# Mixture of experts in token blocks of 32, 32 and 64 instead of 64 and 64, with the first block in four column tiles

## The chip, the cores and the metric

The kernel runs on one core of one Trainium2 chip. The metric is the device time of one execution in microseconds, median of the runs. TensorE (PE) multiplies, VectorE (DVE), ScalarE (ACT) and GpSimd (POOL) work on vectors, SyncE (SP) issues most transfers; each engine runs its own instructions in order, and engines wait for each other by semaphores.

## The reference

One block of a flow model: three parallel token mixers over 256 latent tokens (and 256 context tokens), a merge, a layer norm; then a mixture of experts over the 256 tokens, and another layer norm. Only the mixture is touched here:

```python
def moe_ffn(h, w_router, b_router, w_gate_up, b_gate_up, w_down, b_down):   # h: 256 x 1024
    top_val, top_idx = lax.top_k(h @ w_router + b_router, 4)                # 32 experts
    probs = jax.nn.softmax(top_val, axis=-1)
    ...
    def expert(acc, xs):                                                    # for each of the 32
        gate, up = jnp.split(h @ wgu + bgu, 2, axis=-1)                     # wgu: 1024 x 2048
        gate = jnp.minimum(gate, 7.0)
        up = jnp.clip(up, -7.0, 7.0)
        y = ((up + 1) * gate * jax.nn.sigmoid(1.702 * gate)) @ wd + bd      # wd: 1024 x 1024
        return acc + cw[:, None] * y, None
```

All in f32; the weights of an expert are 12.58 MB. Only a token that chose an expert counts for it. The reference's own inputs send these numbers of tokens to experts 0 to 31 (1,024 in all, 32 on average):

```
17 34 33 47 48  4 19 77   8 46 101 48 28 12 11 40
25  1 46 42 36  8 28 31  44 14  21 64 12 39 32  8
```

So 17 experts have at most 32 tokens, 13 have 33 to 64, experts 7 and 10 have more, and none has over 128.

## The kernel before

The mixers take the first 300 us or so. The rest is a loop over the 32 experts, written out, in the order of the code on every engine (lines 1479 to 1552). The token matrix `h2` stays on the chip. For each expert, 64 slots are filled: `select` (L1359, VectorE) compares each token's place in its expert's list with the slot numbers, `gather` (L1363) multiplies the tokens with this 0/1 matrix on TensorE and scales the product on ScalarE (L1370). Slots for two experts are selected together, two experts ahead.

The expert itself: `gate_up` (L1388) with the slots as the stationary operand, 64 columns, and the weights streaming 512 wide. Two such products, on PSUM partitions 0 to 63 and 64 to 127, form one bank of gate and up; there are two banks (halves 0 and 1 of the hidden size), so two rounds of 16 products. In the trace each f32 product is two records, so a round is 32 records. `act` (L1395) is the clamped SwiGLU of a bank, four VectorE operations and one of ScalarE. `turn` (L1403) transposes the result on TensorE and copies it on ScalarE, `down` (L1410) is 16 products. `spread` (L1416) scales the bank by the tokens' routing weights and splits it in two rounded parts (VectorE, ScalarE, VectorE), and `scatter` (L1421) adds them to the 256 tokens in four PSUM banks, eight products. `spots` (L1373) makes the scatter's matrix and the weights: VectorE scales, TensorE transposes, VectorE compares and sums. It stands between two parts of the second round (L1510). `biases` (L1385) starts each bank with one product. The banks: `gbank` two for gate/up and down, alternating, `sbank` two for everything small.

An expert with over 64 tokens runs a second body, `over`, for 64 more, in two branches (`tc.If`, L1503 `rest_gate` and L1518 `rest`), which TensorE, VectorE and ScalarE skip otherwise. Behind the last expert stands a loop for experts with over 128 tokens (L1557), skipped here.

Weights: SyncE issues them in the order of `queue` (L139 to 145) by `pump` (L148), six transfers of 2 MB per expert (four gate/up, two down), each into a pair of slots of 1 MB. There are 18 slots: 14 in the large arena, two each in `A2` and `A3`. The transfer into a pair waits for the last reader of what was there: `done` frees gate/up pairs 0 and 1 behind the first branch (L1505), pairs 2 and 3 behind the second (L1520), the down pairs in the middle and at the end of `down`. The end of the kernel (L1571 to 1600) takes statistics of the four banks, normalizes and writes four pieces out.

Of the kernel before, what the change touches and what calls it, by code (L numbers as in the profile page):

```python
# [117 lines left out]
def kernel(ctx, tc, x, cx, cols, rows, csts, wsm, wgt, bada, brt, sgub, bdn, bgu,  # L118
# [21 lines left out]
    for e in range(NE):  # L140
        queue += [(("gu", e, i), wgu[e, i]) for i in range(4)]
        if e < NE - 1:
            queue += [(("dn", e, i), wdn[e, i]) for i in range(2)]
        else:
            queue += [(("dn1", e, i), wdn[e, i // 2][:, 2048 * (i % 2):2048 * (i % 2) + 2048]) for i in range(4)]
    loaded = {}

    def pump():  # L148
        while queue:
# [11 lines left out]
            nc.sync.dma_start(out=s, in_=src)  # L161
# [63 lines left out]
    with ExitStack() as p1:  # L225
# [1050 lines left out]
        bgr = Buf(A2, 2, 512)  # L1276
        nc.sync.dma_start(out=bgr[:], in_=bgu.rearrange("p (h n) -> p h n", h=2))
# [6 lines left out]
        bsel = Buf(A2, NE, 2)  # L1284
# [19 lines left out]
        S.copy(out=bst[:], in_=bgr[:])  # L1304
        G.memset(bsel[:], 0.0)
        for r in range(4):
            S.copy(out=bsel[32 * r:32 * r + 32, :, r % 2], in_=ident[32 * r:32 * r + 32, 32 * r:32 * r + 32])
        G.tensor_tensor(out=bst[64:128], in0=bgr[64:128], in1=bst[64:128].bitcast(F32), op=ALU.subtract)
# [36 lines left out]
    def chunk():  # L1345
        return dict(sT=Buf(R, 256), cwv=Buf(A2, 2), gT=Buf(A2, KB, SLOTS), gc=[Buf(A2, 256)])

    yhx, ylx = Buf(R, 512), Buf(R, 512)
    cur, over = chunk(), chunk()
    over["gc"] = over["gc"] + cur["gc"]  # L1350
    cur["gc"] = cur["gc"] + [Buf(A2, 256)]
    ysum = Buf(A2, 512)
    up, sg = ysum[:, 0:256], ysum[:, 256:512]
    sw = ysum[:, 0:256].rearrange("p (t a n) -> p t a n", t=2, a=2)
# [18 lines left out]
    def spots(b, sl, e):  # L1373
        for t in range(2):
            V.tensor_scalar_mul(sw[:, t], sl[:, t, :].unsqueeze(1).to_broadcast([P, 2, SLOTS]), cw[:, t, e:e + 1])
        pw = sps2()
        for t in range(2):
            T.transpose(pw[:, P * t:P * t + P], sw[:, t].rearrange("p a n -> p (a n)"), ident[:])  # L1378
# [3 lines left out]
    def bias_of(e):  # L1382
        V.tensor_copy(out=bse[e % 2][:].rearrange("p (q n) -> p q n", q=2), in_=bsel[:, e, :].unsqueeze(2).to_broadcast([P, 2, SLOTS]))  # L1383

    def biases(e, hf, pg):  # L1385
        mm(pg[:], bse[e % 2][:], bst[:, hf, :], start=True, stop=False, skip_group_check=True)  # L1386

    def gate_up(hT, pg, ks, w):  # L1388
        for k in ks:
            wk = w[k // 2].rearrange("p (k n) -> p k n", k=2)  # L1390
            for q in range(2):
                mm(pg[64 * q:64 * q + 64, :], hT[:, k, :], wk[:, k % 2, 512 * q:512 * q + 512], start=False, stop=k == KB - 1,  # L1392
                   skip_group_check=True)

    def act(b, hf, pg):  # L1395
        gc = b["gc"][hf]
        V.tensor_scalar_min(gc[:], pg[:, 0:256], LIMIT)  # L1397
        S.activation(out=sg[:], in_=gc[:], func=AF.Sigmoid, scale=SW_ALPHA)  # L1398
        V.tensor_scalar(out=up[:], in0=pg[:, 256:512], scalar1=LIMIT, scalar2=-LIMIT, op0=ALU.min, op1=ALU.max)
        V.tensor_tensor(out=gc[:], in0=gc[:], in1=sg[:], op=ALU.mult)  # L1400
        V.scalar_tensor_tensor(out=gc[:], in0=up[:], scalar=1.0, in1=gc[:], op0=ALU.add, op1=ALU.mult)

    def turn(b, hf):  # L1403
# [3 lines left out]
        S.copy(out=b["gT"][:, 4 * hf:4 * hf + 4, :].rearrange("p (q j) n -> p j q n", q=2),  # L1407
               in_=pt[:, 0:256].rearrange("p (j q n) -> p j q n", j=2, q=2))

    def down(b, py, ks, w):  # L1410
        for k in ks:
            wk = w[k // 2].rearrange("p (k n) -> p k n", k=2)
# [66 lines left out]
    for e in range(NE):  # L1479
# [11 lines left out]
        if e:  # L1491
            scatter(cur)
# [188 lines left out]
```

## Time and profile before

| | |
|---|---|
| median of 3 runs | 1285.31 us (1282.2 to 2010.12) |
| the profiled execution | 1286.55 us, its span 1284.7 us |
| TensorE busy | 1189.9 us, 93% |
| TensorE weight loads busy | 611.3 us, 48% |
| VectorE busy | 461.2 us, 36% |
| ScalarE busy | 284.5 us, 22% |
| moved | 471.74 MB, mean 367 GB/s |

Times in the rows are microseconds from the start of the span. A row of the timeline is a run of like instructions: start, time from the first start to the last end, engine, line, operation, tiles (out <- in), shape, count, and in brackets how long the engine had been idle and what ended that. `PE` is a product, `PEq` a branch or the like on TensorE's sequencer, `SPq` an issue of a transfer. `128*64` is the tile of the array that a product uses: rows by columns. `PEclk`, the granted clock, is a mean over a window; 1.00 is 2.4 GHz.

### The profile page before, as it was taken

The page shows a single profiled execution, that of the slowest core. Times are in us where ns is not written, and L with a number is a line of the kernel's source. Part 1 is how long each engine was busy: PE and PEld are TensorE (multiplying, and loading weights), DVE is VectorE, ACT ScalarE, POOL GpSimd, SP SyncE. Part 2 cuts the span into 40 slices and gives each one's busy share as a digit, 9 for nine tenths or more (in the row PEclk, how much of TensorE's full clock was granted, in tenths as well). Part 3 has the DMA queues.
Part 4 walks back from the last instruction along what each step waited for, and adds up shares of the span by engine and source line. Part 5 has one row for each costly group of instructions (what it writes and reads, how often), then busy time and mean ns, then how long its engine had stood idle before and what let it go on. Part 6 is the DMA issues. An engine that isn't in the chain of part 4 may idle for free. (4 is left out here: it accounts for less than half of the span.)

```text
span 1284.7 us, 16504 instructions
## 1 busy us (share of the span) xinstructions
PE 1189.9 (93%) x6619; PEld 611.3 (48%) x6624; DVE 461.2 (36%) x988; ACT 284.5 (22%) x548; POOL 28.3 (2%) x42
## 2 busy tenths in 40 slices
PE   7997999999999999999999999999888999889884
PEld 5897889995333434334433334333333333333321
DVE  6488768796222222222212221222222122212223
ACT  5352745634111111111111111111111111111101
POOL 1000000002000000000000000000000000000000
PEclk9998999998999999999999999999999999999998
DMA  9745648777999999989959999999999999999993
GB/s 389 274 152 204 232 178 296 294 311 297 392 415 427 424 427 427 427 323 429 375 213 387 428 425 427 427 425 427 427 426 426 427 425 427 425 427 426 428 423 149
DMA packets 39470, 471.74 MB, mean 367 GB/s; under 512 B 4529, under 2 KB 4657, under 8 KB 7473
## 3 DMA queue, kind: packets, MB, share of 16 engines
q1 hardware_dynamic: 37008, 463.75, 87.3%
q10 hardware_dynamic: 1696, 4.40, 1.0%
q8 instruction: 89, 1.46, 0.5%
q0 software_dynamic: 640, 1.84, 0.5%
q14 instruction: 37, 0.30, 0.1%
HBM read 468.92 MB, written 1.05 MB: 366 GB/s over the span
## 5 line engine op out<-in xcount | busy, mean ns | idle before, releaser
L1392 PE MATMUL bank<-arena,arena 128*64 128x512 f32 x1808 | 408.8, 596 | 18.3 <-DMA arena<-in_wgu_dram 17.7
L1414 PE MATMUL bank<-arena,arena 128*64 128x512 f32 x1088 | 251.7, 604 | 25.5 <-DMA arena<-in_wdn_dram 17.9
L1392 PEld LDWEIGHTS bank<-arena,arena 128*64 128x64 f32 x1808 | 124.1, 137 | 260.5 <-issue 235.6
L1414 PEld LDWEIGHTS bank<-arena,arena 128*64 128x64 f32 x1088 | 79.3, 138 | 174.8 <-issue 152.7
L246 PE MATMUL bank<-rounded 128*128 128x256 f32 (+1 forms) x1152 | 149.6, 289 | 0.1
L246 PEld LDWEIGHTS bank<-rounded 128*128 128x128 f32 x1152 | 144.0, 195 | 1.8 <-issue 0.6
L1397 DVE TENSOR_SCALAR arena<-bank 128x256 f32<-128x256 f32 x68 | 28.9, 424 | 280.4 <-PE bank L1392 280.4
L1417 DVE SCALAR_TENSOR_TENSOR arena<-bank,arena,g2q 128x512 f32<-128x512 f32 x33 | 24.8, 751 | 271.8 <-PE bank L1414 163.3
L1398 ACT ACTIVATE arena<-arena 128x256 f32<-128x256 f32 x68 | 28.4, 417 | 366.5 <-DVE arena L1397 362.6
L1407 ACT COPY arena<-bank 128x256 f32<-128x256 f32 x68 | 25.3, 372 | 294.4 <-PE bank L1406 294.4
L1392 PE MATMUL bank<-arena 128*64 128x512 f32 x368 | 85.4, 606 | 3.0 <-DMA arena<-in_wgu_dram 2.6
L343 DVE TENSOR_TENSOR rounded<-arena,rounded 128x2048 fp32r<-128x2048 f32 x29 | 66.2, 2284 | 15.1 <-ACT rounded L338 15.1
L1367 PE MATMUL bank<-arena 128*128 128x128 f32 (+1 forms) x576 | 69.9, 275 | 0.7 <-DVE rounded L1383 0.7
L1367 PEld LDWEIGHTS bank<-arena 128*128 128x128 f32 x576 | 66.9, 192 | 1.5 <-ACT arena L1232 0.8
L1370 ACT ACTIVATE arena<-bank,shc 128x128 f32<-128x128 f32 (+1 forms) x144 | 53.3, 450 | 50.7 <-PE bank L1367 50.7
L338 ACT CAST rounded<-arena 128x2048 fp32r<-128x2048 f32 x29 | 55.0, 1898 | 9.2 <-PE bank L246 5.6
L1379 DVE TENSOR_SCALAR rounded<-bank 128x256 fp32r<-128x256 f32 x34 | 14.5, 425 | 117.0 <-PE bank L1378 117.0
L1392 PEld LDWEIGHTS bank<-arena 128*64 128x64 f32 x368 | 25.2, 139 | 53.6 <-issue 45.3
L1418 ACT CAST rounded<-arena 128x512 fp32r<-128x512 f32 x33 | 20.4, 618 | 111.5 <-DVE arena L1417 111.5
L1426 PE MATMUL bank<-rounded 64*128 64x512 f32 x264 | 40.8, 418 | 3.6 <-ACT rounded L1418 3.1
L1426 PEld LDWEIGHTS bank<-rounded 64*128 64x128 f32 x264 | 22.8, 184 | 33.9 <-issue 25.1
L1386 PE MATMUL bank<-rounded 128*128 128x512 f32 x68 | 32.5, 477 | 5.8 <-PEq L1503 3.8
(326 smaller groups left out, 889.5 us busy)
## 6 DMA issues: line engine op xcount, KB each, us to landing
arena<-in_wgu_dram SPq DMA_DIRECT2D x128, 2048.0 KB, 28.7
arena<-in_wdn_dram SPq DMA_DIRECT2D x62, 2048.0 KB, 27.3
arena<-in_win_dram SPq DMA_DIRECT2D x23, 1024.0 KB, 5.3
arena<-in_wada_dram SPq DMA_DIRECT2D x16, 1024.0 KB, 4.9
arena<-in_wad_dram SPq DMA_DIRECT2D x8, 1024.0 KB, 11.1
arena<-in_wbr_dram SPq DMA_DIRECT2D x4, 1024.0 KB, 5.6
arena<-in_wout_dram SPq DMA_DIRECT2D x4, 1024.0 KB, 5.5
arena<-in_wdn_dram SPq DMA_DIRECT2D x4, 1024.0 KB, 33.6
```

Of the source, the lines that this page charges most:

```text
L246: mm(o, l, r, start=start and n == 0, stop=stop and n == len(todo) - 1)
L338: S.copy(out=wh[:, 0:2048], in_=w)
L343: V.tensor_tensor(out=wl[:, 0:2048], in0=w, in1=wh[:, 0:2048].bitcast(F32), op=ALU.subtract)
L1367: mm(pg[:, w * k:w * k + w], h2[:, t, 512 * a + P * k:512 * a + P * k + P], b["sl"][:, t].rearrange("p i n -> p (i n)"), start=t == 0, sto ...
L1370: S.activation(out=b["hT"][:, 4 * a + k].rearrange("p i n -> p (i n)"), in_=pg[:, w * k:w * k + w], func=AF.Identity, scale=shc[:, 1, 4 * ...
L1386: mm(pg[:], bse[e % 2][:], bst[:, hf, :], start=True, stop=False, skip_group_check=True)
L1392: mm(pg[64 * q:64 * q + 64, :], hT[:, k, :], wk[:, k % 2, 512 * q:512 * q + 512], start=False, stop=k == KB - 1, skip_group_check=True)
L1397: V.tensor_scalar_min(gc[:], pg[:, 0:256], LIMIT)
L1398: S.activation(out=sg[:], in_=gc[:], func=AF.Sigmoid, scale=SW_ALPHA)
L1407: S.copy(out=b["gT"][:, 4 * hf:4 * hf + 4, :].rearrange("p (q j) n -> p j q n", q=2), in_=pt[:, 0:256].rearrange("p (j q n) -> p j q n", j ...
L1414: mm(py[64 * q:64 * q + 64, :], b["gT"][:, k, :], wk[:, k % 2, 512 * q:512 * q + 512], start=k == 0, stop=k == KB - 1)
L1426: mm(acc[t][hf][:], b["sT"][sl, P * t:P * t + P], y_[sl, :], start=False, stop=last and y_ is ylx, skip_group_check=True)
```

## The change

Each expert's first 32 tokens (`one`) are done with a stationary operand of 32 columns: four products, on PSUM partitions 0, 32, 64 and 96, each against another quarter of the gate/up weights, 512 wide. One bank then holds gate and up for the whole hidden size, so there is one `act`, one `turn` of 32 x 1024, and `down` runs on four tiles of 32 columns as well. Tokens 33 to 64 (`two`) run the same again on the other bank, in three branches that are skipped otherwise: gate/up with `act` and `spots`; `turn`, `down` and `spread`; the scatter. Tokens 65 to 128 (`over`) stay in 64-column tiles, now in two branches, the gate/up of both halves in the first. All four gate/up pairs are freed behind that branch. `select` for `over` moves into its branch, and `spots` of `one` stands behind the scatter of the expert before. The biases become two products per bank. The weights are laid out anew on the host.

The loop for over 128 tokens moves in front of the last expert, whose gate/up and down weights come in smaller transfers; one `scaled` and one `scatter_whole` end it. The block that makes `cwT` moves from expert 0 to expert 2. At the end one output transfer moves from ScalarE's queue to SyncE's. `A2` gives 1,544 columns to the arena of rounded data; the number of slots is as before.

```diff
     def spots(b, sl, e):
+        m = sl.shape[-1]
         for t in range(2):
-            V.tensor_scalar_mul(sw[:, t], sl[:, t, :].unsqueeze(1).to_broadcast([P, 2, SLOTS]), cw[:, t, e:e + 1])
+            V.tensor_scalar_mul(sw[:, t].rearrange("p (a n) -> p a n", n=m), sl[:, t].unsqueeze(1).to_broadcast([P, P // m, m]),
+                                cw[:, t, e:e + 1])
...
+    def biases(o, pg):
+        for i in range(2):
+            mm(pg[:], o[:], bst[:, i, :], start=i == 0, stop=False, skip_group_check=True)
+
+    def gate_up(hT, pg, w):
+        for k in range(KB):
+            for r in range(4):
+                mm(pg[FEW * r:FEW * r + FEW, :], hT[:, k, :], w[k][:, 512 * r:512 * r + 512], start=False, stop=k == KB - 1,
                    skip_group_check=True)
...
+    def down(b, py, w):
+        for i in range(4):
+            for h in range(2):
+                for q in range(2):
+                    mm(py[64 * q + FEW * h:64 * q + FEW * h + FEW, :], b["gT"][:, 2 * i + h, :], w[i][:, D * h + 512 * q:D * h + 512 * q + 512],
+                       start=i == 0, stop=i == 3)
...
     for e in range(NE):
+        last = e == NE - 1
...
+        if last:
+            scatter(one, yx)
+            room = many([g0, g1])
...
-        gate_up(hT, g0, range(8), w)
-        act(cur, 0, g0)
-        if e:
-            scatter(cur)
+        gate_up(hT[:, :, 0:FEW], g0, w)
+        act(one["gc"][0], g0)
+        with tc.If(tv > FEW):
+            biases(bse[e % 2], g1)
+            gate_up(hT[:, :, FEW:SLOTS], g1, w)
+            act(two["gc"][0], g1)
+            spots(two, sl[:, :, FEW:SLOTS], e)
+        if 0 < e < NE - 1:
+            scatter(one, yx)
+        spots(one, sl[:, :, 0:FEW], e)
...
         with tc.If(tv > SLOTS):
-            rest_gate(e, w)
-        for i in range(2):
-            done(("gu", e, i))
...
+            over_begin(e, 1, [g0, g1])
+            gate_up_over([g0, g1], range(KB), w)
+            over_end(e, [g0, g1])
+        for key in [("gu", e, i) for i in range(4)] if not last else [...]:
             done(key)
         if e % 2 == 0 and e + 2 < NE:
             select(q_["sl"][:], 2, 0, e + 2)
...
         if e + 2 - e % 2 < NE:
             gather(q_, e % 2, 2)
+        with tc.If(tv > FEW):
+            turn(two)
+            py = sps2()
+            down(two, py, wd)
+            spread(two, py, yx)
+            if last:
+                scatter(two, yx)
+        with tc.If(tv > SLOTS):
+            turn(over)
+            py = sps2()
+            down_over(py, wd)
+            spread(over, py, yover)
+            scatter(over, yover)
+        turn(one)
         if e + 1 < NE:
+            bias_of(bse[(e + 1) % 2], bsel[:, e + 1, :])
+        if e + 2 < NE:
+            biases(bse[(e + 1) % 2], g1)
+        down(one, g0, wd)
...
+        if not last:
+            with tc.If(tv > FEW):
+                scatter(two, yx)
+            spread(one, g0, yx)
...
+            scaled(one, g0)
+            scatter_whole(one, True)
...
-    S.dma_start(out=out[0:P, 512:1024], in_=o[0][1])
     stats3(1, 1)
     norm2(0, 0)
+    nc.sync.dma_start(out=out[0:P, 512:1024], in_=o[0][1])
```

## Rows read from the trace of the kernel before

**Rows 1.** The page, part 2: what the transfers moved in 40 equal slices

```profile
GB/s 389 274 152 204 232 178 296 294 311 297 392 415 427 424 427 427 427 323 429 375 213 387 428 425 427 427 425 427 427 426 426 427 425 427 425 427 426 428 423 149
```

**Rows 2.** Timeline of SyncE's queue: start us, us, engine, line, transfer, count

```profile
309.56 0.33 SPq L161 DMA_DIRECT2D arena<-in_wgu_dram  x1
...
321.34 0.33 SPq L161 DMA_DIRECT2D arena<-in_wgu_dram  x1
...
414.31 17.85 SPq L161 DMA_DIRECT2D arena<-in_wgu_dram  x4
...
440.64 17.91 SPq L161 DMA_DIRECT2D arena<-in_wgu_dram  x4
...
892.31 8.57 SPq L161 DMA_DIRECT2D arena<-in_wdn_dram  x2
...
1189.56 8.58 SPq L161 DMA_DIRECT2D arena<-in_wdn_dram  x2
```

**Rows 3.** Windows: us, busy of PE, PEld, DVE, ACT, POOL, granted clock, DMA share, GB/s

```profile
540.00:580.00 40.00, 37.28 (x182) 13.93 (x178) 8.97 (x22) 4.69 (x11) 0.00 (x0) 1.00 0.87 343
620.00:660.00 40.00, 37.25 (x189) 14.78 (x185) 10.29 (x27) 5.86 (x16) 0.00 (x0) 1.00 0.75 302
660.00:700.00 40.00, 39.53 (x192) 15.86 (x193) 7.91 (x19) 6.20 (x15) 0.00 (x0) 0.96 0.78 307
```

**Rows 4.** Timeline, TensorE: the modulation's products in 32-column tiles, and the next product

```profile
19.95 1.07 PE L260 MATMUL bank<-arena 128*32 128x256 f32 x16
20.95 0.50 PE L779 MATMUL bank<-rounded 128*128 128x256 f32 x2
```

**Rows 5.** Timeline, expert 10: the second body, its end, the gather after

```profile
641.57 7.09 PE L1392 MATMUL bank<-arena,arena 128*64 128x512 f32 x32
...
650.13 0.42 DVE L1401 SCALAR_TENSOR_TENSOR arena<-arena 128x256 f32<-128x256 f32 x1
...
652.92 3.65 PE L1414 MATMUL bank<-arena,arena 128*64 128x512 f32 x16 [0.46 <-ACT arena L1407]
...
656.63 0.75 DVE L1417 SCALAR_TENSOR_TENSOR arena<-bank,arena,g2q 128x512 f32<-128x512 f32 x1 [6.07 <-PE bank L1414]
657.47 0.62 ACT L1418 CAST rounded<-arena 128x512 fp32r<-128x512 f32 x1 [4.60 <-DVE arena L1417]
...
659.99 5.35 PE L1414 MATMUL bank<-arena,arena 128*64 128x512 f32 x16
...
665.55 1.95 PE L1367 MATMUL bank<-arena 128*128 128x128 f32 x16
...
667.53 1.50 ACT L1370 ACTIVATE arena<-bank,shc 128x128 f32<-128x128 f32 x4 [1.42 <-PE bank L1367]
```

**Rows 6.** Timeline, expert 8: what VectorE does for `spots`

```profile
568.82 0.48 DVE L1375 TENSOR_SCALAR arena<-arena,cwt 128x128 f32<-128x128 f32 x2 [0.22 <-DVEq L1503]
...
572.86 0.41 DVE L1380 TENSOR_REDUCE arena<-bank 128x1 f32<-128x256 f32 x1
```

**Rows 7.** Timeline: expert 0's first products, gathers of a second body, a scatter

```profile
314.12 7.09 PE L1392 MATMUL bank<-arena,arena 128*64 128x512 f32 x32
...
510.69 3.79 PE L1367 MATMUL bank<-arena 128*128 128x64 f32 x32
...
1248.08 1.21 PE L1426 MATMUL bank<-rounded 64*128 64x512 f32 x8
```

**Rows 8.** Timeline, the end: last gate/up weights, statistics, last root

```profile
1254.32 3.65 PE L1392 MATMUL bank<-arena,arena 128*64 128x512 f32 x16 [0.23 <-DMA arena<-in_wgu_dram]
...
1271.19 1.29 DVE L1576 BATCH_NORM_STATS2 st<-bank 128x6 f32<-128x512 f32 x2 [3.97 <-PEq L1557]
...
1278.60 0.16 DVE L1598 RECIPROCAL rsx<-rsx 128x1 f32<-128x1 f32 x1 [1.89 <-ACT rsx L1579]
```

**Rows 9.** Windows of 5 and 3 us, columns as in rows 3

```profile
660.00:665.00 5.00, 5.00 (x17) 1.45 (x16) 0.00 (x0) 0.00 (x0) 0.00 (x0) 0.66 0.00 0
...
321.00:324.00 3.00, 2.84 (x15) 1.00 (x15) 2.09 (x6) 0.42 (x1) 0.00 (x0) 1.00 0.56 137
```

More of the change, by code (lines that the diff above doesn't have):

```diff
@@ L140 @@
     for e in range(NE):
-        queue += [(("gu", e, i), wgu[e, i]) for i in range(4)]
+        queue += [(("gu", e, i), wgu[e, i]) for i in range(4 if e < NE - 1 else 3)]
         if e < NE - 1:
@@ L144 @@
         else:
+            queue += [(("gu1", e, i), wgu[e, 3][:, 2048 * i:2048 * i + 2048]) for i in range(2)]
             queue += [(("dn1", e, i), wdn[e, i // 2][:, 2048 * (i % 2):2048 * (i % 2) + 2048]) for i in range(4)]
@@ L1283 @@
         bse = [Buf(R, P) for _ in range(2)]
-        bsel = Buf(A2, NE, 2)
+        bso = [Buf(R, P) for _ in range(2)]
+        bsel = Buf(A2, NE, 4)
         alid = Buf(A2, P)
@@ L1395, in act, with bias_of @@
-    def act(b, hf, pg):
-        gc = b["gc"][hf]
-        V.tensor_scalar_min(gc[:], pg[:, 0:256], LIMIT)
[L1398 to L1403, printed above, removed]
+    def bias_of(o, c):
+        n = c.shape[1]
+        V.tensor_copy(out=o[:].rearrange("p (q n) -> p q n", q=n), in_=c.unsqueeze(2).to_broadcast([P, n, P // n]))
@@ L1443, in scatter_whole @@
                 sl = slice(64 * hf, 64 * hf + 64)
-                mm(acc[t][hf][:], b["sT"][sl, P * t:P * t + P].bitcast(F32), y[sl, :], start=False, stop=last, skip_group_check=True)
-    def rest(e, g, wu, wd, end=False):
-        turn(over, 0)
-        biases(e, 1, g)
-        gate_up(over["hT"][:, :, 0, :], g, range(8), wu)
-        act(over, 1, g)
-        py = sps2()
-        down(over, py, range(4), wd)
-        turn(over, 1)
-        down(over, py, range(4, 8), wd)
-        if end:
-            V.scalar_tensor_tensor(out=ysum[:], in0=py[:], scalar=over["cwv"][:, 0:1], in1=g2q[:], op0=ALU.mult, op1=ALU.mult)
-            scatter_whole(over, ysum, False)
-        else:
-            spread(over, py)
-            scatter(over)
+                mm(acc[t][hf][:], b["sT"][sl, P * t:P * t + P].bitcast(F32), ysum[sl, :], start=False, stop=last, skip_group_check=True)
@@ L1518 @@
-        with tc.If(tv > SLOTS):
-            rest(e, g1, wu, wd)
-        for i in range(2, 4):
-            done(("gu", e, i))
-        if e + 1 < NE:
-            bias_of(e + 1)
+            over_begin(e, 1, [g0, g1])
+            gate_up_over([g0, g1], range(KB), w)
+            over_end(e, [g0, g1])
+        for key in [("gu", e, i) for i in range(4)] if not last else [("gu", e, 0), ("gu", e, 1), ("gu", e, 2), ("gu1", e, 0), ("gu1", e, 1)]:
+            done(key)
         if e % 2 == 0 and e + 2 < NE:
@@ L1536 @@
+        with tc.If(tv > SLOTS):
+            turn(over)
+            py = sps2()
+            down_over(py, wd)
+            spread(over, py, yover)
+            scatter(over, yover)
+        turn(one)
+        if e + 1 < NE:
+            bias_of(bse[(e + 1) % 2], bsel[:, e + 1, :])
+        if e + 2 < NE:
+            biases(bse[(e + 1) % 2], g1)
+        down(one, g0, wd)
+        for key in [("dn", e, i) for i in range(2)] if not last else [("dn1", e, i) for i in range(4)]:
             done(key)
-        if e < NE - 1:
-            spread(cur, g0)
+        if not last:
+            with tc.If(tv > FEW):
+                scatter(two, yx)
+            spread(one, g0, yx)
```

203 lines of the change are left out of this document (103 added, 100 removed).

## The prediction

> **What bounds the kernel now.** I first read the 40 slices of the page: the GB/s line stands at about 427 from the thirteenth slice to the last but one, with dips in slices 18 and 20 to 22 [rows 1]. The MoE stage moves 32 experts of 12.58 MB, so it lives off the transfers. Then the queue of SyncE, which issues them. Nine slot pairs of 2 MB exist: the third gate/up pair of expert 1 went out at 309.56, behind the six pairs of expert 0, with nothing released yet, and the fourth only at 321.34 [rows 2]. In the first half the issues come every 26.3 us per expert (414.31 to 440.64): that is TensorE's pace, the pairs being there already. Later ten experts take 297.3 us, 29.7 each [rows 2]: the transfers' pace, 4.97 us per pair. So TensorE and transfers are only 3.4 us apart. Third, the dips, by 40 us windows [rows 3]: against 427 GB/s they lose 7.9 us (540 to 580), 11.7 and 11.2 (620 to 700), 30.8 in all. These are the two experts with over 64 tokens, 7 and 10 by the reference's counts: TensorE works so long that all nine pairs are full and SyncE has nothing to issue. Last, the end: the last gate/up weights of expert 31 are there at 1254.3 [rows 8], 30.4 us before the span's end.
>
> **The change, by kinds of expert.** By the reference's counts 17 experts have up to 32 tokens, 13 have 33 to 64, two have more. Before, all but the two cost TensorE the same 26.3 us. The bytes stay; what changes is TensorE's time per expert and when it lets pairs go. I count from the start of an expert's gate/up work with its weights there.
>
> *Four tiles.* The trace has this shape: 16 records of 128*32 tiles with 256 columns went by in 1.00 us (19.95 to 20.95) [rows 4]. An expert's gate/up work is eight times that: 8.0 us at most; half of the present two times 7.09 [rows 5] is 7.1. I take 7.0, since a change of tile shape is paid once, and 3.6 for down.
>
> *One body (up to 32 tokens).* Gate/up 7.0. Its activation on VectorE ends 1.9 later (650.13 + 0.42 against TensorE's end at 648.66 [rows 5]), `spots` adds 0.5 of scaling [rows 6] and some 0.2 for the branch; the scatter of the expert before, 1.2 us [rows 7], lies beside this. Transposes, the skipped body: all four gate/up pairs are released at 10.3. Gather until ScalarE may start 2.0, its four scaled copies 1.5 [rows 5], the turn's copy 0.4 queued behind them, down 3.6, skips: 18.0. An even expert waits some 1.1 more for `select`, which now stands right ahead of its gather, behind two VectorE operations on the transposes (0.4 each, the second in [rows 6]). Being under 29.7, this kind waits for weights.
>
> *Two bodies (33 to 64).* To the 7.0 come two bias products 0.6 and the second gate/up 7.0: 14.6. Now `spots` of the second half stands straight behind its activation, and TensorE runs in order: it sits idle for 1.9 + 0.5 + 0.1; before, products of the up half lay over that. Transposes, then the scatter that is queued behind them; VectorE's 0.8 on the first transposes and another 0.7 of scaling end after that scatter, then the second transposes: release at 20.0. Gather 2.0, ScalarE 1.5 + 0.4, down 3.6: 27.4. The turn of the first half queues on ScalarE behind the cast of `spread`, which ends 1.5 after that product (656.63 to 658.09 [rows 5]), so down of the first half starts at 29.4 and ends at 33.0; scatter 1.2 and a branch: 34.5. TensorE's own work in this is 28.5, the lower bound; the upper is 38.5, each stretch of waits pulling the clock down (below).
>
> *Over 64.* The 34.5, and: `select` behind VectorE's chain 1.0, two gathers 3.8 (x32 [rows 7]), four bias products 1.1, 64-column products 14.1, transposes 0.5: release at 40.3. The two activations (3.5) hold up ScalarE's turn copies by 2.2; turn 0.9 (0.46 of it idle ahead of 652.92 [rows 5]), 3.6, turn 0.9, 3.6 for down, and the scatter waits for its spread (1.6 and 1.2). That makes 68.8; 71.8 for expert 10, whose `select` waits for both activations. Bounds: 57, TensorE's own work in it, and 72.5.
>
> **The sum.** Expert 0 starts at 314.4, 0.3 later than now (314.12 [rows 7]) for one bias product more. In order, with 34.5 for two bodies, 1.1 for even experts and the `cwT` block of some 3.4 us, which moves from expert 0 to 2: expert 1 starts at 332.2, 2 at 366.7, 3 at 405.7, 4 at 440.2, 5 at 475.8, 6 at 493.8, TensorE is free at 512.9. Expert 7's last gate/up pair is the thirteenth behind the release at 460.2 (expert 4); a queue that ran dry moves again about 1.8 us after the release (issue at 321.34, 137 of 427 GB/s in 321 to 324 [rows 2, 9]), so it lands at 526.6. TensorE has 1.9 of its 7.0 left then, as if it had started at 521. Plus 68.8: 590; then 609 (expert 8), 643.5 (9), 715 (10), 750 (11). The last dry queue is that of expert 11, released at 735: seven pairs on, 735 + 1.8 + 34.8 = 772, expert 13's gate/up is there. From here the transfers set the pace again; 15, 24, 27 and 29 stand alone, and their 34.5 fits into the nine pairs' cover (a release may come 5 x 4.97 = 24.8 after the last gate/up landing). 18, 19 and 20 in a row lose 2. So the last gate/up lands at 772 + 18 x 29.7 + 2 = 1309, against 1254.3 now.
>
> *The end.* Half the down work (minus 3.6), one turn less (0.9), the branch in front of the statistics gone (about half of VectorE's 3.97 us wait, the rest is the scatter [rows 8]), the output's transfer no longer ahead of ScalarE's last root (VectorE's 1.89): 30.4 becomes about 23. That transfer goes to SyncE, behind one that is ready earlier, so nothing waits for it. The tests of the loop for over 128 tokens are made while expert 31's weights land, and its transfers don't run. Span 1332.
>
> *The clock.* After 656.63 TensorE had little to do for 3.4 us, and the next 16 records took 5.35 us instead of 3.65, the granted clock being 0.66 in that 5 us, so mostly at 1.2 GHz [rows 5, 9]: 1.7 us lost. Around the first dip it stayed at 1.00 [rows 3]. The two-body waits (14.6 to 20) are longer. I put half of 1.7 on each of the eight heavy experts up to 11: 7 us. Span 1339. The present execution (1286.55) lies 1.9 above its span (1284.7) and 1.2 above the median (1285.31), so **1340 us**.
>
> The Trainium skill ("TensorEngine Tiling", PSUM Bottleneck) warns that tiling speeds up the products and not what empties the bank behind them. That speaks against this change: the 1.9 us of activation are as long behind 32 tokens as behind 64, and two bodies have them twice.
>
> **The rivals.**
> *The transfers never run dry.* Light experts at 18 us leave slack, nine pairs cover 44 us of transfers, so the dips vanish: minus 30.8; with the end's minus 7: 1247, faster. It needs expert 7 and 10 to let their gate/up pairs go within 24.8 us of the last landing, where I have 40.3 - 5.1 = 35, and experts 1 to 4 (34, 33, 47, 48 tokens) to take under 29.7 each. Chance 0.05.
> *The waits are covered.* If two bodies cost TensorE's bare work, about 29, and the big ones 57 to 60, the same sum has the last landing at 1267: 1290, no change. For it: VectorE and ScalarE are mostly idle. Against: an engine runs in order, and the waits are chains, not load. Chance 0.15.
> *The clock falls in every heavy expert:* 38.5 for two bodies, the last landing at 1343: 1366. For it the 0.66; against, that TensorE had idle stretches in the first dip too and kept 1.00. Chance 0.18. The Trainium skill ("TensorE: Matmul & The Clock Gate", HAM oscillation) describes it: matmuls in bursts shorter than the waits between them run each burst slow. By that rule this rival's time holds; the trace agrees for one of the two dips.
> *Four tiles don't overlap:* gate/up stays at 14, two bodies cost over 50: beyond 1450. The 1.00 us of [rows 4] shows the overlap, so 0.02.
>
> **How the numbers follow.** The forecast has 0.60. Within 2% (what a measurement here can tell from no change) is 1260 to 1311: the covered waits, 0.15. Faster 0.05. Slower 0.60 + 0.18 + 0.02 = 0.80. The range goes from 1300, between forecast and the covered waits, to 1368, every clock drop; the forecast's own is 1318 to 1355.
>
> **What would show it.** The GB/s line should hold more dips than now, in 380 to 470, 550 to 610 and 660 to 740, and hardly any after 750; experts 1 to 4 should start 34 to 39 us apart on TensorE; ahead of the second `spots` transposes TensorE should be idle for about 2.5 us, released by VectorE, and ahead of down by ScalarE; gate/up of 64 records should take 7 us; 13 to 31 should run at 29.7 per expert with TensorE waiting for weights; VectorE's statistics should follow the last scatter at once. I am wrong if experts 1 to 4 run at 30 us or less, or if SyncE doesn't run dry beside experts 7 and 10.

## The result and the profile after

The changed kernel takes 1396.03 us (1389.88 to 1403.67), the kernel before 1284.36 beside it: a ratio of 1.088, interval 1.081 to 1.095. One run of the kernel before, of 2010.12 us, is left out of the ratio. The change makes it slower, as forecast, but by 112 us where I had 55, and above the range. The profiled execution took 1393.32 us, its span is 1391.5, against a forecast span of 1339.

The transfers in 40 equal slices, from the page of the changed kernel (before: [rows 1]):

```profile
GB/s 392 232 187 189 223 228 291 276 364 275 373 316 289 317 425 426 370 173 424 283 242 147 427 425 427 425 423 427 403 345 424 426 426 426 426 426 426 420 362 62
```

A slice is 34.8 us. Slices 11 to 14 (348 to 487 us) are down to 289 to 373, 17 and 18 to 370 and 173, 20 to 22 to 283, 242 and 147: the dips that I forecast, in the forecast places. Slices 29 and 30 (974 to 1044, experts 18 to 20) are deeper than I had, and the last one is nearly empty.

Expert 3 (47 tokens) on TensorE, from the first block's gate/up to the scatter of the second (timeline: start us, us, engine, line, operation, tiles, shape, count, idle time and what ended it):

```profile
420.25 7.07 PE L1401 MATMUL bank<-arena,arena 128*32 128x512 f32 x64
427.25 0.73 PE L1395 MATMUL bank<-rounded 128*128 128x512 f32 x2
427.92 7.07 PE L1401 MATMUL bank<-arena,arena 128*32 128x512 f32 x64
437.17 0.52 PE L1385 MATMUL bank<-ident,arena 128*128 128x128 f32 x2 [2.18 <-DVE arena L1381]
437.62 1.93 PE L1455 MATMUL bank<-rounded 64*128 64x512 f32 x8
439.49 0.69 PE L1385 MATMUL bank<-ident,arena 128*128 128x128 f32 x2
441.12 3.71 PE L1371 MATMUL bank<-arena 128*128 128x128 f32 x16 [0.94 <-DVEq L1559]
444.66 0.38 PE L1420 MATMUL bank<-ident,arena 128*128 128x128 f32 x2
446.74 3.64 PE L1430 MATMUL bank<-arena,arena 128*32 128x512 f32 x32 [1.69 <-ACT arena L1422]
452.84 0.41 PE L1420 MATMUL bank<-ident,arena 128*128 128x128 f32 x2 [2.47 <-DVEq L1576]
453.07 0.73 PE L1395 MATMUL bank<-rounded 128*128 128x512 f32 x2
453.74 3.64 PE L1430 MATMUL bank<-arena,arena 128*32 128x512 f32 x32
457.31 1.20 PE L1455 MATMUL bank<-rounded 64*128 64x512 f32 x8
```

Four tiles do what they promise: 64 records in 7.07 us. The gate/up weights were read by 434.99. Behind that comes the chain of waits: 2.18 for `spots`, 0.94 for the skipped body for over 64 tokens (L1559), 1.69 for the copy of `turn` on ScalarE, 2.47 for VectorE, which has still to pass the other skipped body (L1576). The transfers into this expert's slots, in SyncE's queue (same columns; of the four in the last row only the first is for this expert's slots):

```profile
440.30 0.33 SPq L166 DMA_DIRECT2D arena<-in_wgu_dram  x1
440.72 1.69 SPq L166 DMA_DIRECT2D arena<-in_wdn_dram  x2
442.50 36.62 SPq L166 DMA_DIRECT2D arena<-in_wgu_dram  x4
```

They start 5.3, 5.7 and 7.5 us behind the last product that read the slots, when TensorE was past the skipped body. And the end, experts 30 and 31 on TensorE:

```profile
1331.03 0.53 PE L1385 MATMUL bank<-ident,arena 128*128 128x128 f32 x2 [1.11 <-DVE arena L1381]
1338.55 0.66 PE L1420 MATMUL bank<-ident,arena 128*128 128x128 f32 x2 [7.00 <-PEq L1576]
1339.67 4.94 PE L1430 MATMUL bank<-arena,arena 128*32 128x512 f32 x32 [0.46 <-ACT arena L1422]
1346.27 0.50 PE L1455 MATMUL bank<-rounded 64*128 64x512 f32 x1 [1.66 <-ACT rounded L1447]
1347.00 1.20 PE L1455 MATMUL bank<-rounded 64*128 64x512 f32 x7 [0.23 <-DVE rounded L1448]
1353.84 1.19 PE L1395 MATMUL bank<-rounded 128*128 128x512 f32 x2 [5.65 <-PEq L1488]
1354.97 3.64 PE L1401 MATMUL bank<-arena 128*32 128x512 f32 x16
1358.38 5.84 PE L1401 MATMUL bank<-arena,arena 128*32 128x512 f32 x48
1366.82 0.66 PE L1385 MATMUL bank<-ident,arena 128*128 128x128 f32 x2 [2.60 <-DVE arena L1381]
1370.72 0.66 PE L1420 MATMUL bank<-ident,arena 128*128 128x128 f32 x2 [3.24 <-PEq L1576]
1371.85 5.92 PE L1430 MATMUL bank<-arena,arena 128*32 128x512 f32 x32 [0.46 <-ACT arena L1422]
```

PEq is TensorE's own sequencer. It needs 7.00 us to pass the bodies that expert 30 skips, 5.65 for the loop for over 128 tokens, 3.24 for expert 31's skipped bodies. The last gate/up transfers went out by 1333.2 and land 11.3 us later, about 1344; their expert starts at 1354.97.

What TensorE waited for over the whole span (us in total, times, longest):

```profile
PE bank L1385 <- DVE arena L1381: 54.0, 32, 2.6
PE bank L1420 <- DVEq L1576: 32.1, 13, 2.5
PE bank L1430 <- ACT arena L1422: 26.5, 17, 3.2
PE bank L1420 <- PEq L1576: 25.9, 8, 7.0
PE bank L1401 <- DMA arena<-in_wgu_dram: 19.7, 10, 3.0
```

In all, TensorE waits 121 us at branches, its own or those that another engine has still to pass, against 11 in the kernel before. So two accounts offered themselves. **W**: the waits, and among them the branches, which I had costed at some 0.2 us each. **C**: the low clock. TensorE spent 211.6 us behind 312 us at 1.2 GHz, against 22.5 before (summed from the clock's records).

### The profile page after: what moved, and what is told of

It is laid out like the page before. It is cut to its first block, busy times and chain, and to the rows that moved or that the text cites. A ratio compares the mean times of both kernels' runs of the same rounds, so it can differ in the third digit from the quotient of the medians.

```text
span 1391.5 us, 20301 instructions
## 1 busy us (share of the span) xinstructions
PE 1111.6 (80%) x8214; PEld 588.4 (42%) x8214; DVE 467.1 (34%) x984; ACT 278.2 (20%) x529; POOL 27.3 (2%) x42
## 5 line engine op out<-in xcount | busy, mean ns | idle before, releaser
L1401 PE MATMUL bank<-arena,arena 128*32 128x512 f32 x2528 | 287.7, 602 | 27.0 <-DMA arena<-in_wgu_dram 16.7
L1430 PE MATMUL bank<-arena,arena 128*32 128x512 f32 x1504 | 192.7, 658 | 26.5 <-ACT arena L1422 26.5
L1401 PEld LDWEIGHTS bank<-arena,arena 128*32 128x32 f32 x2528 | 79.3, 111 | 221.1 <-issue 193.8
L1443 DVE SCALAR_TENSOR_TENSOR arena<-bank,arena,g2q 128x512 f32<-128x512 f32 x49 | 36.8, 751 | 391.2 <-PEq L1591 159.5
L1371 PE MATMUL bank<-arena 128*128 128x128 f32 (+1 forms) x576 | 98.0, 341 | 41.4 <-DVE arena L1363 14.5
L1371 PEld LDWEIGHTS bank<-arena 128*128 128x128 f32 x576 | 91.6, 250 | 49.3 <-issue 46.7
L1430 PEld LDWEIGHTS bank<-arena,arena 128*32 128x32 f32 x1504 | 47.1, 120 | 148.7 <-issue 102.9
L1420 PE MATMUL bank<-ident,arena 128*128 128x128 f32 x102 | 24.7, 330 | 72.5 <-DVEq L1576 32.1
L1455 PE MATMUL bank<-rounded 64*128 64x512 f32 x384 | 65.2, 453 | 8.2 <-ACT rounded L1447 4.8
L1385 PE MATMUL bank<-ident,arena 128*128 128x128 f32 x98 | 27.7, 361 | 54.1 <-DVE arena L1381 54.0
L1401 PE MATMUL bank<-arena 128*32 128x512 f32 x480 | 60.0, 619 | 6.8 <-PEq L1591 3.9
L1455 PEld LDWEIGHTS bank<-rounded 64*128 64x128 f32 x384 | 37.7, 201 | 44.2 <-issue 29.9
L1420 PEld LDWEIGHTS bank<-ident,arena 128*128 128x128 f32 x102 | 13.0, 164 | 91.6 <-ACTq L1576 56.7
L1385 PEld LDWEIGHTS bank<-ident,arena 128*128 128x128 f32 x98 | 14.0, 156 | 87.6 <-DVE arena L1381 78.6
```

Source lines behind the costliest of these rows:

```text
L1371: mm(pg[:, w * k:w * k + w], h2[:, t, 512 * a + P * k:512 * a + P * k + P], b["sl"][:, t].rearrange("p i n -> p (i n)"), start=t == 0, sto ...
L1385: T.transpose(pw[:, P * t:P * t + P], sw[:, t], ident[:])
L1401: mm(pg[FEW * r:FEW * r + FEW, :], hT[:, k, :], w[k][:, 512 * r:512 * r + 512], start=False, stop=k == KB - 1, skip_group_check=True)
L1430: mm(py[64 * q + FEW * h:64 * q + FEW * h + FEW, :], b["gT"][:, 2 * i + h, :], w[i][:, D * h + 512 * q:D * h + 512 * q + 512], start=i == ...
L1443: V.scalar_tensor_tensor(out=ysum[:], in0=py[:], scalar=b["cwv"][:, 0:1], in1=g2q[:], op0=ALU.mult, op1=ALU.mult)
L1455: mm(acc[t][hf][:], b["sT"][sl, P * t:P * t + P], y_[sl, :], start=False, stop=False, skip_group_check=True)
```

## The experiments

All ratios are to the kernel before, run beside it.

**1. Branches or clock.** Without branches, the counts `CNT` being written into the program (`SLOTS` likewise, and no loop over 128):

```diff
-        with tc.If(tv > FEW):
+        if CNT[e] > FEW:
```

> The branches of the changed kernel are replaced by the known counts of tokens when the kernel is written: what an expert does not need is not in the program, and the loop for experts with over 128 tokens is left out. So no engine skips anything, and an expert with few tokens no longer waits behind a body that it does not run (its bank, its engines). W (waits behind skipped bodies and the skips themselves, 25.9 us on TensorE at one branch, 14.0 at another, 32.1 of waits of the first turn for VectorE's branch) says that the 56 us by which I was too low go: 1340 to 1350. C (the low clock of TensorE, 212 us of it after 312 us against 23 before) says that the waits of the two-body experts stay, and the clock with them: 1375 or more.

Measured: 1346.58 us, 1.049 (1.046 to 1.052), 49.5 less, with about as much time at the low clock (219.6 us). W holds. Then zeros on TensorE in its waits, `n` products at each place:

```diff
+        idle2(acc[0][0][:], n)
         pw = sps2()
```

> The changed kernel with products of zeros on TensorE where it waits (nine ahead of the second block's transposes in spots, four ahead of each other spots, four ahead of and six behind each gather, three ahead of the first block's down), so that it is busy in the waits; each is 0.21 us at 2.4 GHz and 0.43 at 1.2. C says that the clock stays high and the time falls to 1355 to 1370, though the products themselves take up to some 4 us per expert. W says no gain: the waits stay, the time is within 10 us of the changed kernel's 1396.

> Both: no branches (and no loop for over 128 tokens, so part of the program is left out), and products of zeros in TensorE's waits. If waits and clock add, this is the sum of the two gains: W with C says below 1330. If the clock falls only because of the waits behind branches, it is the same as without branches alone.

Measured: 1402.3 (1.092; 1.089 to 1.095) and 1344.08 (1.047; 1.043 to 1.050). The time at the low clock fell from 211.6 to 100.0 us, and from 219.6 to 69.6, and neither time moved by more than its interval. C falls as an explanation of the 56 us: 49.5 of them went with the branches while the low clock stayed, and raising it in this way gives nothing back. That it would give nothing if it cost nothing isn't shown, since the products of zeros take time too.

**2. The bank of the turn.** One more turn of the two small banks:

```diff
+        sps2()
         turn(one)
```

> The changed kernel with the two small banks turned once more ahead of the first block's turn, so that this turn no longer writes the bank that the gather for the experts two ahead, and the skipped body's product, use. W says that the wait of TensorE at this turn (1.6 for ScalarE's copies, 2.5 for VectorE's branch) becomes shorter where it is the bank that it waits for: 10 to 20 us less than 1396. C says nearly the same time, since the wait moves to the next dependency.

Measured: 1409.42, 1.098 (1.091 to 1.104). It is not less. The row of waits shows why: instead of VectorE's branch the same turn now waits for ScalarE's.

```profile
PE bank L1420 <- ACTq L1576: 48.3, 27, 2.2
```

So the turn is held by the engines that must come past the skipped body first; another bank only changed which one is last.

**3. Which branches.** Without the loop for over 128 tokens (its `with tc.If(most > 2 * SLOTS)` deleted):

> The changed kernel without the loop for experts with over 128 tokens, which stands in front of the last expert (left out; no expert here has so many). Everything else, the other branches too, stays. In the changed kernel TensorE waited 7.0 us at 1338.55 and 5.65 at 1353.84 beside this loop, and expert 30 took 33.5 us instead of about 21. W, with the cost of passing a large skipped body: 10 to 14 us less, 1382 to 1386. If expert 31's start is set by its weights, nothing: 1396.

Measured: 1401.02 (1395.36 to 1406.67), 1.092 (1.080 to 1.103). No gain, so a miss. The wait of 7 us that I had put down to the loop is still there, the loop being gone:

```profile
1358.37 0.66 PE L1420 MATMUL bank<-ident,arena 128*128 128x128 f32 x2 [7.11 <-PEq L1551]
```

It belongs to expert 30's skipped bodies. The loop's own 5.65 us are gone from this trace, but its queue ran dry longer in the first half (last gate/up weights some 20 us later than in the profiled execution of the changed kernel), and two runs that lie 11 us apart can't separate that. Then all skipped bodies, the taken ones still branches:

```diff
-        with tc.If(tv > FEW):
+        if CNT[e] > FEW:
+            with tc.If(tv > FEW):
```

> The changed kernel with each branch that would be skipped left out of the program (by the known counts), while every branch that is taken is still a branch, and the loop for over 128 tokens still stands in front of the last expert. If the price lies in skipped bodies (TensorE's walk past them and the waits for engines that are still to pass them): experts with up to 32 tokens at 17 to 19 us instead of 20 to 25, and 20 to 30 us less in all, 1366 to 1376. If it lies in every branch, taken or not: less than 10 us less, above 1385.

Measured: 1360.76, 1.060 (1.052 to 1.068): 35 of the 49.5 come back. Of the price that is left, the loop is 11.11 us of TensorE's time between experts 30 and 31:

```profile
1323.16 1.22 PE L1395 MATMUL bank<-rounded 128*128 128x512 f32 x2 [11.11 <-issue]
```

By the bytes moved, the last gate/up weights land here when they do without any branch (1319.1 us in both traces), and the 10.0 us between the two spans lie behind that.

**4. What a skipped body does.** Only one kind of skipped body is left out in each:

> The changed kernel in which the two branches for over 64 tokens are left out of the program for the 30 experts that skip them (by the known counts); all other branches stay, and the loop for over 128 tokens too. The first of these skipped bodies reads all four gate/up pairs. In the changed kernel SyncE's transfers into the pairs of expert 3 (gate/up read until 434.99) went out at 440.72 and 442.50, when TensorE had passed that branch; without branches each pair went out as its last product was read. Theory R (the skipped reader holds the pairs): two-body experts let their pairs go 6 to 7 us earlier for the last and 12 for the first, the last gate/up weights land 15 to 25 us earlier: 1370 to 1380. Theory S (what costs is only TensorE's own walk past bodies, of which there are fewer): its waits at the turn behind these bodies go for all experts, but those on the second block's branches stay: within 10 us of 1396.

> The complement: the three branches for the second block are left out for the 17 experts with up to 32 tokens; the branches for over 64 tokens stay for all. Theory R: light experts have slack, the pairs of the two-body experts are held as before: 1385 to 1396. Theory S: the light experts lose three of their five skips, 15 to 25 us less: 1371 to 1381.

Measured: 1372.32, 1.067 (1.061 to 1.072), and 1391.38, 1.084 (1.081 to 1.087). The totals fall where theory R has them; its way there is only half right. Expert 3 in the first of the two, TensorE and then SyncE's queue:

```profile
416.94 7.08 PE L1401 MATMUL bank<-arena,arena 128*32 128x512 f32 x64
...
424.61 7.07 PE L1401 MATMUL bank<-arena,arena 128*32 128x512 f32 x64
```

```profile
426.59 0.33 SPq L166 DMA_DIRECT2D arena<-in_wgu_dram  x1
428.31 2.04 SPq L166 DMA_DIRECT2D arena<-in_wdn_dram  x2
431.74 0.33 SPq L166 DMA_DIRECT2D arena<-in_wgu_dram  x1
```

The second gate/up ends at 431.68, and the four pairs go one by one as it runs. In the changed kernel they went from 440.30 to 442.50, for an expert that started at 420.25 instead of 416.94: 20.1 to 22.3 us behind the start there, 9.7 to 14.8 here. So the skipped body is a reader of the four pairs like any other, and holds them until TensorE has come past it. That part of R is shown.

What it is worth is not. By the bytes moved, the last gate/up weights of expert 5 land 14.8 us earlier than in the changed kernel, but those of expert 31 only 5.2, where R had 15 to 25. The other 18 of the 23.4 us between the two spans lie behind that landing, where the walks of 7.00 and 3.24 us are gone. The lead at expert 5 is gone by expert 11. Experts 7 and 10 take 75.7 and 79.8 us here, with 20.5 and 23.9 us of it at the low clock; in the changed kernel's execution 68.5 and 72.1, with 3.4 each. In the complement the landing is 6.7 us later and the rest 8.7 shorter. With both kinds out (experiment 3) the landing is 23.0 earlier; without any branch (experiment 1) it is 23.1 earlier, and for expert 5 already 23.4. So the two don't add up, and how the 35 us divide between held pairs, waits and walks stays open.

**5. The wait in `spots`.** Its scaling moved ahead of gate/up, its transposes ahead of the activation:

```diff
+        spots_scale(sl[:, :, 0:FEW], e)
         gate_up(hT[:, :, 0:FEW], g0, w)
+        if 0 < e < NE - 1:
+            scatter(one, yx)
+        spots_turn(one)
         act(one["gc"][0], g0)
```

> The changed kernel with the scaling of spots ahead of gate/up and its transposes, comparison and sum ahead of the activation, for the first block (its scatter ahead of that too) and for the second. So TensorE no longer waits about 2 us for VectorE behind each gate/up (54.0 us in 32 waits in the changed kernel), and lets the four gate/up pairs go earlier. If that wait delays the end, 32 of those us stand in experts 0 to 11, where weights are released too late: 15 to 30 us less, 1366 to 1381. If the wait only moves to the turn behind it: within 8 us of 1396.

> The same move of spots in the kernel without branches (1346.6; the loop for over 128 tokens left out as there). Without branches nothing behind the transposes has to wait for other engines, so the gain should come through: 15 to 25 us less than 1346.6, so 1322 to 1332. If the waits move to the turn behind it, 1340 or more.

Measured: 1373.64, 1.070 (1.065 to 1.076), and 1322.38, 1.030 (1.025 to 1.036): 22 and 24 us less, both as expected. This wait was in my sum (1.9 + 0.5 + 0.1 a block), and it was real time. Not all of the 54.0 us came back: with the branches kept, TensorE's idle time ahead of the gather (L1371) rose from 41.4 to 89.8 us. It adds to the branches: 1396.0 - 49.5 - 22.4 = 1324.1, and both together take 1322.4.

**6. A mixed kernel.** Four tiles for light experts, before's 64 columns and order for the others; in the second run the `if` is a branch with two arms:

```diff
+        if CNT[e] > FEW:
+            biases(bso[0], g0)
+            gate_up_half(hT, g0, 0, range(8), w)
...
+        else:
...
+            gate_up(hT[:, :, 0:FEW], g0, w)
```

> A kernel that takes from each side what the runs showed to be cheap: experts with up to 32 tokens in four tiles of 32 columns (16 to 17 us in the kernels without branches), experts with 33 to 64 in one body of 64 columns in the order of the kernel before (26.3 us there), over 64 as in the changed kernel; spots early for the light ones, select ahead of gate/up. The choice is made by the known counts when the program is written, and the loop for over 128 tokens is left out. Theory (the transfers run dry because two bodies in a row hold the gate/up pairs too long, and nothing else is wrong with four tiles): TensorE is ahead of the transfers from expert 5 on, the queue is dry only beside experts 7 and 10, some 8 us each, last gate/up weights at about 1215, end 27 us later: 1240 to 1260, faster than before. Rival (four tiles or the late release of all four pairs cost by themselves): 1280 or more.

> The same, with the choice made on the chip by the count of tokens (two branches per expert with two arms each, a third inside for over 64 tokens, and the loop for over 128 tokens behind the last expert): nothing is left out. Each engine passes one arm per branch. If skipped bodies cost what they cost in the changed kernel (2 to 4 us per expert, up to 7 for TensorE at one place) they are hidden in the transfers' 29.5 us per expert except at the end: 1255 to 1275, faster than before by 1 to 2%. If passing a large arm holds TensorE or the queue of releases more than that: 1285 or more.

Measured: 1289.78, 1.003 (1.002 to 1.005), and 1336.88, 1.041 (1.037 to 1.044). Both miss. In the first, TensorE waits 126 us in all for gate/up weights, so it is ahead of the transfers, and still nothing is gained:

```profile
PE bank L1407 <- DMA arena<-in_wgu_dram: 68.4, 34, 3.0
PE bank L1442 <- DMA arena<-in_wgu_dram: 57.3, 26, 3.0
```

Against a queue that lands a pair every 4.92 us, its landings from about the tenth to the last gate/up pair come 49 us late in sum, those of the kernel before 35 (worked out, to about 1 us, from the bytes of the transfers' records; the sums in the expectations take in the last output too). With the gate/up weights laid out by k, all four pairs stay in use until an expert with over 64 tokens has finished its gate/up. To test that in the kernel before, pairs 0 and 1 are given back with 2 and 3:

```diff
-        for i in range(2):
-            done(("gu", e, i))
```

> The kernel before with one step of the change alone: gate/up pairs 0 and 1 are freed together with pairs 2 and 3, behind the second branch, so some 10 us later in an expert with up to 64 tokens and some 28 us later in experts 7 and 10. Theory (what the change loses beyond its waits is the late release beside the long experts): two more pairs, 10 us of transfers, are missing beside each of 7 and 10: 1300 to 1315. Rival (the time at which pairs come free does not matter so long as TensorE is as fast): 1283 to 1290.

Measured: 1285.12, 1.001 (0.999 to 1.002). This run doesn't test the theory. SyncE's issues stand as far apart as before (29.39 us for the four gate/up pairs from 536.63, against 29.37 from 538.91): the transfer waits for the last reader, wherever the program gives the slot back. To free a pair later one has to read it later, and the other way round, so the layout of before again and `over`'s first half ahead of the second half of the 64:

```diff
+                gate_up_half(over["hT"][:, :, 0, :], pg, 0, range(6), w)
```

> The mixed kernel without branches (1289.8; the choice is made by the known counts when the program is written, and the loop for over 128 tokens is left out), but with the gate/up weights in the layout of the kernel before, half by half, and with its order for over 64 tokens: gate/up pairs 0 and 1 are freed behind the first half. Theory of late release: it lost 63.3 us against a queue that never runs dry, nearly all beside experts 7 and 10; with two pairs freed 20 us earlier at each, 20 us of it come back: 1262 to 1275, faster than before. Rival: 1284 or more, if TensorE with four tiles reads pairs 2 and 3 so late that nothing is gained.

Measured: 1259.99 (1258.15 to 1262.46), 0.982 (0.980 to 0.984): faster than both kernels, and a little more than expected. The landings come 19 us late in sum instead of 49, which is the 30 us between the two times. That the earlier release alone did it isn't shown: the new order also makes the long experts themselves shorter, expert 7 from 79.3 to 65.7 us and expert 10 from 69.8 to 59.4 (from start to start on TensorE), with 10.2 and 0.0 us of low clock instead of 17.1 and 13.7. Its transfers:

```profile
GB/s 389 287 152 211 225 190 283 293 300 338 384 426 428 426 429 426 428 349 429 414 264 420 427 427 428 428 428 427 427 428 427 428 427 427 428 428 427 427 424 190
```

It is a kernel for these counts alone. What the kernel before would gain from having its own branches written out by the counts wasn't run, so the 1.8% aren't shown to be the four tiles'. With the choice on the chip, in one branch of two arms per expert, and in two:

> The mixed kernel in the layout of the kernel before (1260.0 with the counts known when the program is written), now with the choice made on the chip: one branch per expert with two arms that hold the whole expert, two branches inside for over 64 tokens, the loop for over 128 tokens behind the last expert; nothing is left out. In the mixed kernel with two branches per expert the choice on the chip cost 47 us (1336.9 against 1289.8). If the price goes by the number of branches: about half of it, 1280 to 1290. If it goes by the instructions that are passed: as much as with two, 1300 or more. If it hides in the transfers' time: 1262 to 1275, faster than before by 1% or more.

> The same kernel with two branches per expert (gate/up, and down), each with two arms. If the price goes by the number of branches: some 47 us, 1300 to 1310, and 20 to 25 more than with one. If it goes by the instructions passed, the same time as with one branch within 8 us.

Measured: 1307.83, 1.018 (1.016 to 1.020), and 1322.34, 1.029 (1.027 to 1.031). One branch costs 48 us over none, the second 14.5 more, which lies between the two expectations. So the number of branches isn't what sets most of the price. That it is the length of what is passed is argued, not shown: the 48 also hold the loop for over 128 tokens and the two inner branches, and no run separates them; 40 of them lie ahead of the last gate/up landing. With one branch, TensorE stands between two experts, ahead of the next one's first product (L1401; "issue" is time in which it waited for nothing that the profile shows):

```profile
PE bank L1401 <- issue: 70.9, 16, 9.2
```

No changed or mixed kernel with the choice on the chip beats the kernel before.

**7. The end's edits alone**, in the kernel before:

```diff
-    S.dma_start(out=out[0:P, 512:1024], in_=o[0][1])
     norm2(0, 0)
+    nc.sync.dma_start(out=out[0:P, 512:1024], in_=o[0][1])
```

> The kernel before with only the end's edits of the change: the last expert's fourth gate/up transfer in two, its last down transfer in two smaller ones, and one output transfer from ScalarE's queue to SyncE's, behind one that is ready earlier. I costed the last at 1.89 us of VectorE's wait: 1281.5 to 1284 against some 1285, a ratio of 0.997 to 0.999. Rival (another wait takes its place at the end): 1.000.

Measured: 1282.9 (1280.06 to 1283.83), 0.9988 (0.9976 to 1.0000): some 2 us, as costed, with an interval that reaches to no change. The run holds the smaller last transfers too, so the 2 us aren't the output's move alone.

## Why the prediction was right in direction and wrong in size

The span was 1391.5, I had 1332 before adding 7 for the clock: 59.5 too little. Of these about 35 lie ahead of the last gate/up landing (1344 against 1309) and about 24 behind it (47 against 23). Most of the 35 are there early: expert 7 starts at 544.0 where I had TensorE free at 512.9. Of these 31 us, 18.7 are in experts 0, 5 and 6 with one body (25.4, 24.2 and 24.0 us against 17.8, 18.0 and 19.1; without branches 20.2, 16.9 and 19.9), and 11.0 in experts 1 to 4 (39.1, 40.0, 38.2 and 37.3 against 34.5, 39.0, 34.5 and 35.6; without branches 37.2, 39.9, 36.0 and 36.8).

- **Four tiles.** 7.07 for 64 records against 7.0. Right.
- **One body, 18.0 and 19.1.** Without branches 16.9 and 19.9 (experts 13 and 12). In the changed kernel 20.3 to 20.7 where the clock stays high, up to 25.4 elsewhere. The step that failed is "skips", at 0.2 each: where the changed kernel's clock stays high they cost expert 12 0.8, expert 8 2.4 and expert 13 3.4 us, and experts 0, 5 and 6, at the low clock in part, 4.1 to 7.3, by the waits of the gather and the turn for engines that have still to pass them. In the kernel before 0.2 a skip is about what TensorE's waits there show (below the list); why its skipped bodies cost so much less isn't shown.
- **Two bodies, 34.5, upper bound 38.5.** Measured from start to start 37.0 to 40.0 in experts 1 to 4, 9 and 11; without branches 35.6 to 37.2, expert 2 with its `cwT` block left aside. The chain was the right one: 2.18 for `spots`, the turn behind `spread`. What I left out is the 2.47 for VectorE at L1576, 0.94 at L1559, and the gather at 3.71 instead of 2.0, at the low clock.
- **Over 64, 68.8 and 71.8.** Measured 68.5 and 72.1, with 3.4 us of low clock each. Right, and in part luck, as the time holds only at that clock: six other kernels with the same bodies in the same order (experiments 1 to 4, those with zeros aside) took 73 to 81 for them, with 14 to 24 us of it.
- **The release, 10.3, 20.0 and 40.3.** Expert 3's pairs went from 20.1 to 22.3 us behind its start, as costed. Leaving the skipped body out would have let them go from 9.7 on.
- **The last dry queue at expert 11.** It ran dry beside 18 to 20 too: two landings 1.6 and 6.3 us late (pairs of experts 20 and 21), where I had put 2 for all.
- **The end, 23.** Failed. "The tests of the loop are made while expert 31's weights land" supposed that TensorE waits for them. TensorE was the later one: 7.00 and 5.65 us of passing put expert 31's start at 1354.97, 11 us behind its weights, and then 3.24 more, and gate/up and down at the low clock (9.25 and 5.92 us instead of 7.07 and 3.64). The smaller claims hold: the statistics follow the scatter at once, at 1379.87, and VectorE's 1.89 [rows 8] is gone.
- **The clock, 7 us.** There is far more of it than I took (211.6 us), so the rival in which it falls in every heavy expert was nearer in size, 1366. Raising it with zeros gave nothing, and without branches 49.5 us went while it stayed, so nothing shows that it is what the forecast lacked. But it falls in one trace and not in the next for the same work, and experts 7 and 10 take 4 to 12 us longer where it does. The rule that the prediction names with that rival, bursts shorter than the waits between them, does not fit these experts: gate/up runs for 7.07 us, and the wait behind it is 2.18.
- **The rivals.** The largest wait that stood against "the waits are covered" is the one in `spots`: moving it gives 22 us with the branches kept, and leaves the kernel 84 above that rival's 1290.

TensorE's waits at the two skipped branches of the kernel before, over the whole span (us in total, times, longest):

```profile
PE bank L1414 <- PEq L1518: 6.1, 19, 0.4
PE bank L1386 <- PEq L1503: 3.8, 23, 0.2
```

Had the branches been free, the time would have come out near my sum: the same kernel without them and without the loop takes 1346.6 against 1340, lands its last gate/up weights at about 1321 (1309), and ends 25 us later (23). Its span of 1345.8 is 14 above my 1332; experts 7 and 10 alone, at 80.5 and 76.1 us with 23.9 and 13.7 of low clock, are 16 above what I had for them.

The Trainium skill ("Runtime: NRT & Kernel Launch", Instruction fetch mechanics) says that a taken branch whose target lies outside the pages already fetched waits for a fetch of the target. The traces fit it. In the records of the transfers, a packet of 16 KB on a queue of instruction fetches (q8 on the page) ends 1.6 to 1.8 us before TensorE goes on in the stands of 7.00, 5.65, 3.24, 7.11 and 11.11 us shown above; for the 7.00 it runs from 1335.72 to 1336.74, and TensorE goes on at 1338.55. In the kernel with one branch per expert it ends 1.5 to 1.7 us before, in each of the 14 stands of over 4 us ahead of an expert's first product. Whose instructions these packets hold, and what fills the 4.2 us of the 7.00 before the packet starts, no run here shows. Their number says little, since a shorter program needs fewer: 118 in the changed kernel, 89 in the kernel before, 64 without branches.

## What to carry to other kernels

Don't price a skipped body as a test, and don't carry its price over from another kernel: buffers that it reads stay in use until the engine has come past it, and other engines' waits gather behind it. TensorE's waits at one were 0.4 us at most in the kernel before and up to 7.00 in the changed one. A kernel that lives off its transfers may gain nothing from faster products on its busiest engine, as the first mixed kernel did not; look at when the last reader of each buffer comes, above all beside the longest piece of work. And move work that doesn't depend on the product ahead of it, so that an in-order engine doesn't stand behind it.

## What the runs showed of the hardware

- TensorE stood 2.15 to 7.00 us, eight times, behind skipped bodies of the second block and for over 64 tokens in the changed kernel (25.9 us in all), and up to 9.2 us between two experts in the kernel with one branch of two arms per expert.
- In each of the stands of 3.24 us and more shown above, and in the 14 of over 4 us in the one-branch kernel, a 16 KB packet of instructions had landed 1.5 to 1.8 us before TensorE went on.
- A transfer went out 0.06 us behind the end of the last product that read its slots (431.68 to 431.74) where no branch stood between them.
- The same 32 gather products in expert 10, at a granted clock of 1.00 (2.4 GHz) in the changed kernel and of 0.50 (1.2 GHz) in the kernel without skipped bodies for over 64 tokens, behind nearly the same wait:

```profile
690.36 3.79 PE L1371 MATMUL bank<-arena 128*128 128x64 f32 x32 [1.05 <-DVE arena L1363]
```

```profile
686.33 7.09 PE L1371 MATMUL bank<-arena 128*128 128x64 f32 x32 [1.04 <-DVE arena L1363]
```
